# Gated-delta/pool decoder step: squares before norming, later roots, and another place for one weight block

## The chip, the cores and the metric

The kernel runs on one core of one Trainium2 chip. The metric is the device time of one execution in microseconds (us), as a median over runs; lower is better. Five engines of the core matter: TensorE (PE in the profile, with PEld for its weight loads), VectorE (DVE), ScalarE (ACT), GpSimd (POOL) and SyncE (SP), which only issues loads. Each works off its own list of instructions in order, and semaphores hold an instruction back until what it needs is there.

## The reference

One decoder layer runs over 512 prompt tokens and 8 sample tokens. A combined projection feeds a gated delta net and a pooling group, an output projection `W_out` adds to the residual `h`, and then comes the part at which the change sits:

```
h   = h + concat(dn_out, pool_out) @ w_out
xn2 = h * rsqrt(mean(h*h) + EPS) * norm_ffn         # RMSNorm over 2048 features
gu  = xn2 @ w_gate_up                               # 2048 -> 2 x 5632
h   = h + (silu(gu[:, :5632]) * gu[:, 5632:]) @ w_down
```

## The kernel before

**Layout and products.** Features lie on the 128 partitions, the 520 tokens along the free axis in two halves of 260. The residual stands in two tiles of eight feature rows each, `mixa` (the first 1024 features) and `mixb` (the others), `part(hk, half, ...)` picking tile and token half. Each float32 operand is split into a high part `hi` and a low part `lo` (`hi` is a cast on ACT, L1217 or L1535; `lo` a subtraction on DVE, L1218 or L1539). A product of one weight block (1024 x 128) with one form (1024 features x 260 tokens) is `passes`: eight steps of three matmuls (hi·hi, hi·lo, lo·hi, L1224 to L1226), so 24 matmuls of 128x260. A form that changes place in eight rows is made by `stream`: four pairs of rows, each with a DVE operation, a cast on ACT and a subtraction on DVE.

**The stages around the change.** The output projection ends with an output pair called `last`. Its second token half is finished from the banks `acc_c[0]` and `acc_c[1]`: `finish` (L1562) adds a bank to the residual (L1559, DVE), squares it (L1565, ACT) and stores it (L1566, a DMA on ACT's queue), and `total` (L1570, DVE) adds the squares to `sqa`. All squares share one buffer, so each square waits for the sum before it. For RMSNorm, `roots` (L1378) lets PE sum `sqa` over the partitions (L1383), DVE scale it (`sv`, L1387) and POOL take the power -1/2 (L227); `diagonals` (L1395, DVE, three pieces) and `spread` (L1401 on PE, L1402 on ACT) spread the result over partitions as `rb2`; `normed` (L1413, DVE) multiplies two rows of a half by it. `weighted` (L1408, ACT) puts the norm's weight on the last rows.

Then the gate and up projections begin. Pairs are `gu[0]` (gate, blocks `w0`) and `gu[1]` (up, blocks `w1`), called pair 0 and pair 1 here, each with blocks A11, A21, A12 and A22. They are worked off in plain products while the seven forms B11, B21, B22, T1, T2, T3 and T4 are built from the normed halves; from `gu[2]` on Strassen's seven products per pair run (M1, M4, M7, M6, M5, M2, M3 in this order). Of these, M4 is the first to read the form T4, with block A22 of `gu[2]`; M7 needs the sum block S3, for which A21 of `gu[2]` is loaded into rows of `mixb`, once the first cut of T4 has read them.

**Order.** No scheduler works here (`manual_schedule`): the order of the lines is the order on each engine.

**Places.** Blocks cut by `cut` go to the rotating tiles `hi`/`lo` of the pool `wpl` (three each), or to another pool if one is named. Pair 0's A22 is cut into the pool `sc0`, and before the change so is pair 1's A22, after it. `place` (L1527) instead writes the two parts of a block side by side into one tile of an old form. The old T4 of the output projection (`t4oh`, `t4ol`, pool `t4p`) holds pair 0's A11 and A21 in this way. When the plain products are issued, `p2a`, `sc0` and `t4p` are closed, and the new T4's high tile `T4h` is laid at bytes 129,728 to 138,048 of each partition; `sc0`'s high tile begins at 137,952, so that the two share 96 bytes. Its low tile `T4l` takes the place of `t4ol`. `t4oh` shares no byte with either.

Of the kernel before, what the change touches and what calls it, by code (L numbers as in the profile page):

```python
# [69 lines left out]
def decoder_kernel(ctx, tc, x_prompt, x_sample, state_delta, state_conv, state_pool, norm_mix, w_in,  # L70
# [17 lines left out]
    def pst():  # L88
        return ps_dn.tile([P, 512], F32, tag="dn", name="dn")
# [70 lines left out]
    def weights(view, K, parts=None):  # L160

        ng = -(-K // HG)
        sizes = [K // ng + (1 if i < K % ng else 0) for i in range(ng)]
        out = []
        k0 = 0
        for n in sizes:
            hi, lo = granule(view, k0, n, P, parts)
            for j in range(n):
                out.append((hi[:, j, :], lo[:, j, :]))
            k0 += n  # L170
        return out
# [38 lines left out]
    def part(hk, half, k0=0, k1=8):  # L210
        return (mixa, mixb)[hk][:, k0:k1, HALF * half:HALF * half + HALF]
# [54 lines left out]
    with tc.tile_pool(name="ph0", bufs=2) as ph0, tc.high_priority(offset=10 * AHEAD), tc.manual_schedule():  # L266
# [20 lines left out]
        def roots(ti, parts=1):  # L287
            s, r = ss0[:, 2 * ti:2 * ti + 1], rs0[:, ti:ti + 1]
            if parts == 2:
                dve.tensor_tensor(s, s, ss0[:, 2 * ti + 1:2 * ti + 2], op=ALU.add)  # L290
            dve.tensor_scalar(s, s, 1.0 / D, EPS, op0=ALU.mult, op1=ALU.add)
            pow_mhalf(r, s)
# [11 lines left out]
        class Block:  # L304
# [24 lines left out]
            def high(self):  # L329
                act.copy(self.hi, self.xm)  # L330

            def low(self, eng):
                eng.tensor_tensor(self.lo, self.xm, self.hi.bitcast(F32), op=ALU.subtract)  # L333
# [184 lines left out]
    with ExitStack() as p1:  # L518
# [625 lines left out]
        w = weights(w_out[0].rearrange("(k p) c -> p k c", p=P)[:, :, 8 * P:9 * P], KT)  # L1144
# [26 lines left out]
    def stacked(name, bufs=1, side="left"):  # L1171
        stack = ExitStack()
        return stack, stack.enter_context(tc.tile_pool(name=name, bufs=bufs, side=side, reuse_waits="tile"))
# [3 lines left out]
    def form_tiles(pool_, name):  # L1177
        return tuple(pool_.tile([P, 8, HALF], F32R, name=name + x) for x in "hl")

    b11, b21 = form_tiles(f12, "b11"), form_tiles(f12, "b21")  # L1180
    t4s, t4p = stacked("t4p", side="right")
    sc0s, sc0 = stacked("sc0", side="right")
# [7 lines left out]
    forms = {"B11": (xh[:, 0:8, 0:HALF], xl[:, 0:8, 0:HALF]), "B21": (xh[:, 8:16, 0:HALF], xl[:, 8:16, 0:HALF]),  # L1190
             "B22": (xh[:, 8:16, HALF:], xl[:, 8:16, HALF:]), "T1": (xh[:, 0:8, HALF:], xl[:, 0:8, HALF:]),
             "T2": b11, "T3": b21, "T4": form_tiles(t4p, "t4o")}
# [28 lines left out]
    def passes(acc, w, form, start=True, stop=True, ks=None):  # L1221
        (wh, wl), (xf, xg) = w, forms[form]
        for k in ks or range(wh.shape[1]):
            te.matmul(acc, wh[:, k, :], xf[:, k, :], start=start and k == 0, stop=False)  # L1224
            te.matmul(acc, wh[:, k, :], xg[:, k, :], start=False, stop=False)  # L1225
            te.matmul(acc, wl[:, k, :], xf[:, k, :], start=False, stop=stop and k == wh.shape[1] - 1)  # L1226
# [113 lines left out]
    def ffn_pair(fp, up):  # L1340
        return Pair(lambda i, j: wgv[:, 8 * j:8 * j + 8, up * FF + (2 * fp + i) * P:up * FF + (2 * fp + i + 1) * P],
                    up_out if up else gate_out)

    gu = [ffn_pair(fp, up) for fp in range(FP) for up in range(2)]
# [47 lines left out]
    def diagonals(rv):  # L1392
        dg = p2a.tile([P, HALF], F32, tag="dg", name="dg", bufs=1)
        for j, (t0, n) in enumerate(((0, P), (P, P), (2 * P, HALF - 2 * P))):
            dve.tensor_scalar(dg[:, t0:t0 + n], ident[:, P - n:P], rv[:, j:j + 1], None, op0=ALU.mult)  # L1395
        return dg
# [7 lines left out]
    def weighted(half):  # L1404

        for k in (6, 7):
            x = part(1, half)[:, k, :]
            act.activation(x, x, AF.Copy, scale=nffn(8 + k))  # L1408

    def normed(hk, half, k0, k1, eng=dve):  # L1410

        x, rb = part(hk, half, k0, k1), rb2[:, HALF * half:HALF * half + HALF]
        eng.tensor_tensor(x, x, rb.rearrange("p (o c) -> p o c", o=1).broadcast_to([P, k1 - k0, HALF]), op=ALU.mult)  # L1413
# [109 lines left out]
    acc_a, acc_b, acc_c = ([pst()[:, :HALF] for _ in range(2)] for _ in range(3))  # L1523
    w = last.w

    def place(pair, name, hold):

        hi, lo = (hold.rearrange("p k c -> p (k c)")[:, j * HG * P:(j + 1) * HG * P] for j in range(2))
        raw = pair.raw[name]
        act.copy(hi, raw)  # L1530
        dve.tensor_tensor(lo, raw, hi.bitcast(F32), op=ALU.subtract)
        pair.w[name] = [x.rearrange("p (k c) -> p k c", c=P) for x in (hi, lo)]
# [8 lines left out]
    def stream(name, src, make, lag=1):  # L1541

        for i in range(4 + lag):
            if i < 4:
                make(2 * i)
                high(name, src, 2 * i)
            if i >= lag:
                low(name, src, 2 * (i - lag))
# [8 lines left out]
    def add_to(i, half, acc):  # L1557
        x = mix[KT - 2 + i][:, HALF * half:HALF * half + HALF]
        dve.tensor_tensor(x, x, acc, op=ALU.add)  # L1559

    def finish(i, half, acc):
        c = slice(HALF * half, HALF * half + HALF)  # L1562
        add_to(i, half, acc)
        sq = p2.tile([P, NTOK], F32, tag="sq", name="sq")[:, c]
        act.activation(sq, mix[KT - 2 + i][:, c], AF.Square)  # L1565
        act.dma_start(h_d[KT - 2 + i][:, c], mix[KT - 2 + i][:, c])  # L1566
        return sq, c

    def total(sq, c):
        dve.tensor_tensor(sqa[:, c], sqa[:, c], sq, op=ALU.add)  # L1570
# [26 lines left out]
    gu[0].load("A22")  # L1597
    passes(acc_c[1], w["A21"], "T1", stop=False, ks=range(5, 8))
    passes(acc_c[0], w["A12"], "B22", start=False)
    forms["B11"] = b11  # L1600
    stream("B11", part(0, 0), lambda k: normed(0, 0, k, k + 2))
    gu[1].cut("A21")
    gu[1].load("A12")
    total(*finish(0, 1, acc_c[0]))
    passes(acc_c[1], w["A22"], "B22", start=False)
    f1 = finish(1, 1, acc_c[1])
    for k in (0, 2):
        normed(1, 0, k, k + 2)
    total(*f1)
    weighted(1)  # L1610

    xs_.close()
# [10 lines left out]
    def two():  # L1623
        return [pst()[:, :HALF] for _ in range(2)]

    c0 = [ps_mm.tile([P, HALF], F32, tag="mm", name="mm") for _ in range(2)]
    a0 = two()
    halves = slice(0, HALF), slice(HALF, NTOK)
    w0, w1 = gu[0].w, gu[1].w
    passes(a0[0], w0["A11"], "B11", ks=range(5))  # L1630
    rv = roots(1)
    for k in (4, 6):
        normed(1, 0, k, k + 2)
    passes(a0[0], w0["A11"], "B11", ks=range(5, 8))
    passes(a0[1], w0["A21"], "B11", ks=range(6))
    dg = diagonals(rv)
    spread(1, dg)
    for k in range(0, 8, 2):
        high("B21", part(1, 0), k)
        low("B21", part(1, 0), k)  # L1640
    passes(a0[1], w0["A21"], "B11", ks=range(6, 8))
    gu[0].cut("A12")
    gu[1].load("A22")
    a1 = two()
# [26 lines left out]
    stream("T3", part(0, 1), minus(part(0, 1), part(1, 1), part(0, 1)))  # L1671
    gu[1].cut("A12")
    gu[2].load("A22")
    passes(c0[0], w0["A12"], "B22", start=False)
    passes(c0[1], w0["A22"], "B22", start=False)
    stream("T2", part(1, 1), minus(part(1, 1), part(1, 1), part(0, 0)))
    for j in range(2):
        gate_out(j, 1, sg[:, j, halves[1]], c0[j])
    gu[2].cut("A11")
    gu[1].cut("A22", sc0)  # L1680
    h1 = two()
    passes(h1[0], w1["A12"], "B21")
    passes(c1[0], w1["A12"], "B22", start=False)
# [257 lines left out]
```

## Time and profile before

| | us |
|---|---|
| median of 3 runs (2198.1 to 2200.36) | 2199.5 |
| the profiled execution | 2196.74 |
| its span | 2195.0 |
| PE busy in the span | 2149.0 (98%) |
| DVE busy | 1735.2 (79%) |
| ACT busy | 955.0 (44%) |
| POOL busy | 462.9 (21%) |
| mean granted TensorE clock, as a share of full speed | 0.993 |

The span runs from the first to the last instruction; the execution's own time is 1.74 us longer. Times within the profile are in us from the span's start. The change lies between 795 and 885. A timeline row gives the start, the duration, the engine, the line, what is written from what, and in brackets the idle time before it with its inferred releaser.

### The profile page before, as it was taken

Reading aid. Unit: us, or ns where it says so; the run is one execution under the profiler, and the core shown is the slowest. Engines: PE = TensorE matmul, PEld = TensorE weight load, DVE = VectorE, ACT = ScalarE, POOL = GpSimd, SP = SyncE. Lnnn points to the kernel's source line nnn. Section 1 sums busy time; section 2 is a strip of 40 time slices with the busy share of each in tenths; the row PEclk is TensorE's granted clock in tenths of the full one; section 3 lists DMA queues with packets and bytes.
Section 4 is the critical chain, followed back from the end, with each engine's and each line's share of the span. In section 5 each row is a group of like instructions: output and inputs, shape, how many; then the busy total and the mean of one; then the engine's idle time right before and its main releaser. Section 6 shows DMA issues by size and latency. Waiting matters only on the chain.

```text
span 2195.0 us, 42970 instructions
## 1 busy us (share of the span) xinstructions
PE 2149.0 (98%) x17815; PEld 2141.4 (98%) x17815; DVE 1735.2 (79%) x2518; ACT 955.0 (44%) x1491; POOL 462.9 (21%) x520
## 2 busy tenths in 40 slices
PE   5999999999999998999999999999999999999998
PEld 5999999999999998999999999999999999999997
DVE  6676567566489968988898888888887798887996
ACT  5434453443255444433443433434434434435454
POOL 4111111001022210423323333232012402003110
PEclk8999999999999999999999999999999999999999
DMA  6443333323435442545455445545446837438333
GB/s 202 133 105 103 82 82 104 101 76 85 131 105 164 147 131 57 174 142 160 143 150 169 146 137 163 152 136 151 132 135 180 254 101 208 114 103 246 91 108 111
DMA packets 444728, 297.03 MB, mean 135 GB/s; under 512 B 26548, under 2 KB 424653, under 8 KB 441189
## 3 DMA queue, kind: packets, MB, share of 16 engines
q1 hardware_dynamic: 426661, 225.13, 36.3%
q0 software_dynamic: 16880, 68.51, 9.7%
q8 instruction: 139, 2.28, 0.4%
q10 hardware_dynamic: 992, 0.66, 0.1%
q14 instruction: 56, 0.46, 0.1%
HBM read 251.47 MB, written 43.43 MB: 134 GB/s over the span
## 4 chain that ended last, share of the span: by engine, by line
PE 92%; DVE 3%; ACT 1%; issue 1%; DMA 1%; POOL 0%; DVEq 0%; ACTq 0%
PE dn L1224 22%; PE dn L1225 22%; PE dn L1226 22%; PE mm L179 7%; PE mm L181 7%; PE mm L180 7%; PE dn L854 1%; DVE lo L1218 1%; ACT hi L1217 0%; PE dn L1849 0%; PE dn L774 0%; PE dn L964 0%; PE dn L900 0%; PE dn L861 0%; PE dn L836 0%
## 5 line engine op out<-in xcount | busy, mean ns | idle before, releaser
L1217 ACT CAST hi<-raw 128x1024 fp32r<-128x1024 f32 (+1 forms) x425 | 430.6, 1027 | 406.1 <-DVE raw L1246 211.2
L1218 DVE TENSOR_TENSOR lo<-raw,hi 128x1024 fp32r<-128x1024 f32 (+1 forms) x425 | 532.2, 1272 | 91.4 <-ACT hi L1217 89.7
L179 PE MATMUL mm<-xh,hi 128*128 128x256 f32 (+1 forms) x1280 | 379.7, 297 | 0.6 <-ACT ccs L735 0.6
L180 PE MATMUL mm<-xl,hi 128*128 128x256 f32 (+1 forms) x1280 | 362.1, 283 | 2.6 <-DVE xl L333 1.8
L181 PE MATMUL mm<-xh,lo 128*128 128x256 f32 (+1 forms) x1280 | 362.5, 283 | 0.2 <-DVE lo L148 0.2
L180 PEld LDWEIGHTS mm<-xl,hi 128*128 128x128 f32 x1280 | 242.9, 190 | 2.9 <-issue 1.9
L179 PEld LDWEIGHTS mm<-xh,hi 128*128 128x128 f32 x1280 | 242.6, 190 | 1.4 <-ACT ccs L735 0.7
L181 PEld LDWEIGHTS mm<-xh,lo 128*128 128x128 f32 x1280 | 241.7, 189 | 0.4 <-DVE lo L148 0.4
L1226 PE MATMUL dn<-b21h,lo 128*128 128x260 f32 x636 | 180.1, 283 | 0.9 <-DVE lo L1218 0.9
L1224 PE MATMUL dn<-b21h,hi 128*128 128x260 f32 x636 | 180.1, 283 | 0.0
L1225 PE MATMUL dn<-b21l,hi 128*128 128x260 f32 x636 | 179.5, 282 | 0.3 <-DVE b21l L1733 0.3
L1246 DVE TENSOR_TENSOR raw<-raw 128x1024 f32<-128x1024 f32 (+1 forms) x132 | 176.0, 1333 | 2.2
L1226 PE MATMUL dn<-b11h,lo 128*128 128x260 f32 x620 | 175.4, 283 | 0.0
L1224 PE MATMUL dn<-b11h,hi 128*128 128x260 f32 x620 | 175.4, 283 | 0.0
L1225 PE MATMUL dn<-b11l,hi 128*128 128x260 f32 x620 | 174.9, 282 | 0.0
L148 DVE TENSOR_TENSOR lo<-raw,hi 128x1024 fp32r<-128x1024 f32 (+1 forms) x86 | 102.6, 1197 | 75.0 <-ACT hi L146 74.9
L1224 PE MATMUL dn<-T1h,hi 128*128 128x260 f32 x564 | 160.2, 284 | 0.0
L1225 PE MATMUL dn<-T1l,hi 128*128 128x260 f32 x564 | 159.9, 284 | 0.0
L1224 PE MATMUL dn<-B22h,hi 128*128 128x260 f32 x564 | 159.8, 283 | 0.0
L1225 PE MATMUL dn<-B22l,hi 128*128 128x260 f32 x564 | 159.5, 283 | 0.0
L1226 PE MATMUL dn<-T1h,lo 128*128 128x260 f32 x564 | 158.9, 282 | 0.0
L1226 PE MATMUL dn<-B22h,lo 128*128 128x260 f32 x564 | 158.5, 281 | 0.0
(578 smaller groups left out, 6425.3 us busy)
## 6 DMA issues: line engine op xcount, KB each, us to landing
raw<-in_w_gate_up_dram SPq DMA_DIRECT2D x134, 512.0 KB
raw<-in_w_in_dram SPq DMA_DIRECT2D x80, 512.0 KB
a_d<-mixa POOLq DMA_DIRECT2D x22, 1040.0 KB, 5.5
mixb<-in_w_gate_up_dram SPq DMA_DIRECT2D x42, 512.0 KB
raw<-in_w_down_dram SPq DMA_DIRECT2D x48, 448.0 KB
raw<-in_w_out_dram SPq DMA_DIRECT2D x25, 512.0 KB
st<-a_d POOLq DMA_DIRECT2D x49, 260.0 KB, 6.4
raw<-in_w_down_dram SPq DMA_DIRECT2D x24, 512.0 KB
```

Source lines behind the costliest of these rows:

```text
L148: dve.tensor_tensor(lo[:, :f], raw[:, :f], hi[:, :f].bitcast(F32), op=ALU.subtract)
L179: te.matmul(acc[ci], wh, hi[k][:, c0:c1], start=(k == 0), stop=False)
L180: te.matmul(acc[ci], wh, lo[k][:, c0:c1], start=False, stop=False)
L181: te.matmul(acc[ci], wl, hi[k][:, c0:c1], start=False, stop=(k == len(w) - 1))
L854: te.matmul(yp[:, ck(c)], xt_[:, ck(c)], cur[:, ck(c)], start=True, stop=True)
L1217: act.copy(hi, raw)
L1218: dve.tensor_tensor(lo, raw, hi.bitcast(F32), op=ALU.subtract)
L1224: te.matmul(acc, wh[:, k, :], xf[:, k, :], start=start and k == 0, stop=False)
L1225: te.matmul(acc, wh[:, k, :], xg[:, k, :], start=False, stop=False)
L1226: te.matmul(acc, wl[:, k, :], xf[:, k, :], start=False, stop=stop and k == wh.shape[1] - 1)
L1246: dve.tensor_tensor(r[name], r[a], r[b], op=op)
```

## The change

Three things change.

1. In the second half of the output projection's last pair, both `finish`/`total` steps come before pair 1's A21 is cut and before any norming of half 1 of B21; the cut, the load of A12 and one norming step (two rows) follow. One norming step moves behind the request for the roots.
2. The request for the roots of half 1 comes after all eight steps of the product A11·B11 of pair 0, not after five; the spreading of the result after seven steps of the next product, not six.
3. Pair 1's A22 is written into `t4oh` by `place`, ahead of the building of T2, not cut into `sc0` after it.

```diff
-    forms["B11"] = b11
+    forms["B11"], held = b11, forms["T4"]
     stream("B11", part(0, 0), lambda k: normed(0, 0, k, k + 2))
+    total(*finish(0, 1, acc_c[0]))
+    passes(acc_c[1], w["A22"], "B22", start=False)
+    total(*finish(1, 1, acc_c[1]))
     gu[1].cut("A21")
     gu[1].load("A12")
-    total(*finish(0, 1, acc_c[0]))
-    passes(acc_c[1], w["A22"], "B22", start=False)
-    f1 = finish(1, 1, acc_c[1])
-    for k in (0, 2):
-        normed(1, 0, k, k + 2)
-    total(*f1)
+    normed(1, 0, 0, 2)
     weighted(1)
...
-    passes(a0[0], w0["A11"], "B11", ks=range(5))
+    passes(a0[0], w0["A11"], "B11")
     rv = roots(1)
-    for k in (4, 6):
+    for k in (2, 4, 6):
         normed(1, 0, k, k + 2)
-    passes(a0[0], w0["A11"], "B11", ks=range(5, 8))
-    passes(a0[1], w0["A21"], "B11", ks=range(6))
+    passes(a0[1], w0["A21"], "B11", ks=range(7))
     dg = diagonals(rv)
     spread(1, dg)
...
-    passes(a0[1], w0["A21"], "B11", ks=range(6, 8))
+    passes(a0[1], w0["A21"], "B11", ks=range(7, 8))
...
     gu[1].cut("A12")
     gu[2].load("A22")
+    place(gu[1], "A22", held[0])
...
     gu[2].cut("A11")
-    gu[1].cut("A22", sc0)
```

On DVE, from the end of the form B11 to the pieces of the diagonal (`lo<-raw,hi` is pair 1's A21, `sqa` the sum of squares, `rb_7798` the spread roots of half 0):

```order
 L1539 TENSOR_TENSOR b11l<-mixa,b11h 128x520 x2
-L1218 TENSOR_TENSOR lo<-raw,hi 128x1024
 L1559 TENSOR_TENSOR mixb<-mixb,dn 128x260
 L1570 TENSOR_TENSOR sqa<-sqa,sq 128x260
 L1559 TENSOR_TENSOR mixb<-mixb,dn 128x260
-L1413 TENSOR_TENSOR mixb<-mixb,rb_7798 128x2x260 x2
 L1570 TENSOR_TENSOR sqa<-sqa,sq 128x260
+L1218 TENSOR_TENSOR lo<-raw,hi 128x1024
+L1413 TENSOR_TENSOR mixb<-mixb,rb_7798 128x2x260
 L1387 TENSOR_SCALAR sv<-dn 128x3
-L1413 TENSOR_TENSOR mixb<-mixb,rb_7798 128x2x260 x2
+L1413 TENSOR_TENSOR mixb<-mixb,rb_7798 128x2x260 x3
```

Three operations leave the way to the second sum; two of them now stand between it and `sv`, and one more between `sv` and the diagonal.

On ACT, from the casts of T3 to those of T4 (`hi<-raw` are casts of weight blocks, `t4oh<-raw` that of pair 1's A22):

```order
 L1535 CAST T3h<-mixa 128x520 x4
 L1217 CAST hi<-raw 128x1024
+L1530 CAST t4oh<-raw 128x1024
 L1535 CAST T2h<-mixb 128x520 x4
 L1335 ACTIVATE sg<-sg 128x260 x2
-L1217 CAST hi<-raw 128x1024 x2
+L1217 CAST hi<-raw 128x1024
 L1535 CAST T4h<-mixb 128x520 x4
```

One cast moves ahead of T2's; the count of instructions ahead of T4's casts stays the same. On DVE the block's subtraction moves in the same way.

## Rows read from the trace of the kernel before

**Rows 1.** The page: busy time, share of the span and instructions of each engine.

```profile
PE 2149.0 (98%) x17815; PEld 2141.4 (98%) x17815; DVE 1735.2 (79%) x2518; ACT 955.0 (44%) x1491; POOL 462.9 (21%) x520
```

**Rows 2.** Stretches: from:to, length, then PE, PEld, DVE, ACT, POOL busy; PEclk; DMA.

```profile
960.00:1200.00 240.00, 240.00 (x1996) 239.90 (x1995) 209.32 (x221) 95.81 (x118) 76.37 (x60) 1.00 0.51 150
...
808.00:814.00 6.00, 6.00 (x29) 6.00 (x29) 2.00 (x6) 1.02 (x2) 1.17 (x1) 0.50 0.01 3
...
52.00:56.00 4.00, 2.63 (x19) 2.34 (x20) 0.09 (x1) 1.39 (x4) 2.11 (x3) 1.00 1.07 287
```

**Rows 3.** Timeline of PE, 795 to 883: start, duration, instruction, idle before and releaser.

```profile
807.10 1.17 PE L1383 MATMUL dn<-ones,sqa 128*128 128x2 f32 x6 [3.97 <-DVE sqa L1570]
...
814.12 0.64 PE L1401 MATMUL dn<-dg,ones 128*128 128x260 f32 x2
...
828.81 0.39 PE L1225 MATMUL mm<-T1l,t4oh 128*128 128x260 f32 x1 [0.24 <-DVE T1l L1539]
...
851.95 0.39 PE L1226 MATMUL dn<-b21h,lo 128*128 128x260 f32 x1 [0.94 <-DVE lo L1218]
...
862.62 0.39 PE L1224 MATMUL dn<-T4h,hi 128*128 128x260 f32 x1 [2.03 <-ACT hi L1217]
...
865.88 0.59 PE L1226 MATMUL dn<-T4h,lo 128*128 128x260 f32 x1 [2.75 <-DVE lo L1218]
...
881.73 0.28 PE L1226 MATMUL dn<-B22h,lo 128*128 128x260 f32 x1
```

**Rows 4.** Timeline of DVE, 800 to 810: the sums and the roots of half 1.

```profile
800.85 1.48 DVE L1539 TENSOR_TENSOR b11l<-mixa,b11h 128x520 fp32r<-128x520 f32 x2
...
803.72 0.42 DVE L1559 TENSOR_TENSOR mixb<-mixb,dn 128x260 f32<-128x260 f32 x1
804.62 0.43 DVE L1570 TENSOR_TENSOR sqa<-sqa,sq 128x260 f32<-128x260 f32 x1 [0.48 <-ACT sq L1565]
...
806.53 0.42 DVE L1570 TENSOR_TENSOR sqa<-sqa,sq 128x260 f32<-128x260 f32 x1
808.30 0.16 DVE L1387 TENSOR_SCALAR sv<-dn 128x3 f32<-128x3 f32 x1 [1.35 <-PE dn L1383]
...
809.81 0.62 DVE L1395 TENSOR_SCALAR dg<-ident,rv 128x128 f32<-128x128 f32 x3
```

**Rows 5.** Timeline of ACT, 801 to 858.

```profile
801.50 1.04 ACT L1217 CAST hi<-raw 128x1024 fp32r<-128x1024 f32 x1
...
805.48 0.42 ACT L1565 ACTIVATE sq<-mixb 128x260 f32<-128x260 f32 x1 [0.89 <-DVE mixb L1559]
...
808.12 1.17 ACT L1408 ACTIVATE mixb<-mixb,prm 128x260 f32<-128x260 f32 x2 [2.22 <-DMA h_d<-mixb]
...
857.78 1.15 ACT L1535 CAST T4h<-mixb 128x520 fp32r<-128x520 f32 x2 [7.33 <-PE dn L1226]
```

**Rows 6.** Timeline of DVE, 842 to 882: T2, T4 and the blocks of gu[2].

```profile
842.12 1.30 DVE L1553 TENSOR_TENSOR mixb<-mixb,mixa 128x520 f32<-128x520 f32 x2
843.51 0.70 DVE L1539 TENSOR_TENSOR T2l<-mixb,T2h 128x520 fp32r<-128x520 f32 x1
...
851.81 1.30 DVE L1553 TENSOR_TENSOR mixb<-mixb 128x520 f32<-128x520 f32 x2
858.43 0.70 DVE L1539 TENSOR_TENSOR T4l<-mixb,T4h 128x520 fp32r<-128x520 f32 x1 [5.32 <-ACT T4h L1535]
...
863.13 1.22 DVE L1246 TENSOR_TENSOR mixb<-raw,mixb 128x1024 f32<-128x1024 f32 x1 [0.77 <-DMA mixb<-in_w_gate_up_dram]
...
864.61 1.22 DVE L1218 TENSOR_TENSOR lo<-raw,hi 128x1024 fp32r<-128x1024 f32 x1
...
879.72 2.36 DVE L1218 TENSOR_TENSOR lo<-raw,hi 128x1024 fp32r<-128x1024 f32 x2 [1.43 <-ACT hi L1217]
```

**Rows 7.** The chain that ended last: start, length and what, loads alone.

```profile
859.16 3.94 DMA mixb<-in_w_gate_up_dram
...
1743.30 7.10 DMA raw<-in_w_down_dram
```

## The prediction

> **What bounds the kernel now.** I read the page's engine table first: PE is busy for 2149.0 of 2195.0 us [rows 1], so only time that PE loses can be won. Over a steady stretch it runs 1996 matmuls in 240 us without a gap, one per 0.120 us, at the full clock of 2.4 GHz [rows 2]. Then I read PE's timeline where the change sits, for gaps. There are five [rows 3]: 3.97 us before the sums over `sqa` at 807.10, 0.24 at 828.81 (T1's low part), 0.94 at 851.95 (pair 1's A22, low part), and 2.03 and 2.75 in M4, at 862.62 and 865.88 (block A22 of `gu[2]`, high and low part). After the first gap the granted clock is 0.50 (the level of 1.2 GHz): 29 matmuls take 6.00 us [rows 2]. So two places lose time: the roots of half 1, and the start of M4. Each is the end of a chain over DVE and ACT, so the question is how much earlier these chains end.
>
> **Part 1, the squares and the roots.** PE asks for the sums before DVE has made them. Before, the second sum starts at 806.53, and PE follows 0.57 us later [rows 3, 4]. Ahead of the sums DVE has a block's low part and two norming steps, which now come after.
>
> The new chain on DVE: B11 ends at 800.85 + 1.48 = 802.33 [rows 4]. From the first addition to its sum of squares it takes 804.62 - 803.72 = 0.90, the square on ACT included. The sum itself takes 0.43 and then the second addition begins, since one buffer serves all squares. So the second sum starts at 802.33 + 0.90 + 0.43 + 0.90 = 804.56, and PE's sums at about 805.13.
>
> PE arrives there when? Its gap began at 807.10 - 3.97 = 803.13, after five of eight steps; three more steps are nine matmuls of 0.120, or 1.08 us, so it arrives at 804.21. A gap of 0.9 us stays, where 3.97 was.
>
> But DVE now has two operations ahead of `sv`. ACT casts A21 after the second square, which ends near 804.5; the cast takes 1.04 [rows 5], so DVE's subtraction runs from about 805.6 for 1.22 (the same form at 864.61 [rows 6]), to 806.8. One norming step takes 0.65 (half of 1.30, by the like form of T2 at 842.12 [rows 6]), to 807.45, and then comes `sv`. The way from `sv` to the diagonal over POOL took 809.81 - 808.30 = 1.51 [rows 4], to about 809.0; meanwhile DVE norms three times, 1.95, to 809.55. The diagonal takes 0.62, and PE spreads at about 810.2. In the x2 rows neighbours overlap by about 0.1 us, over some five places 0.4 us; I take 810.0. It was 814.12 [rows 3].
>
> PE itself is there earlier: sums of at most 1.17 us and 21 matmuls at 0.120 (2.52) give 808.8, so it waits 1.2 us for the diagonal, a gap which it did not have. It costs nothing beyond 810.0, as DVE and ACT set what follows: T1, through `rb2`, follows the spreading at the same distance as before, and PE already waited 0.24 for T1 [rows 3]; it now waits about 0.7, as three matmuls fewer lie between. **Term 1: 814.1 - 810.0 = 4.1 us**, with 3.4 (if the roots' way over POOL or the cast is slower by half a us) and 4.6 (all overlaps for the good) as ends. ACT's weighting now stands behind the cast; it starts 808.12 - 805.48 = 2.64 after the second square, when the store has landed [rows 5], so at about 806.8, ends near 808, and ACT copies `rb2` after 810: two us of cover. The load of pair 1's A12 waits for A21's raw tile, some 3 us longer against its old place; its cast comes after those of T1, B22 and T3, later than 828.81 [rows 3], so some 20 us on.
>
> **Part 2, pair 1's A22.** The block's cast (1.04) and subtraction (1.22) are not new, only earlier, between T3 and T2, so both engines have the same work ahead of T4. The 0.94 at 851.95 goes. What matters is T4. ACT's first cast of T4 waited 7.33 us until PE had ended, to 857.78 [rows 5]; that end is the last product with pair 1's A22, since `T4h` shares 96 bytes with the tile in which that block lay. DVE had been ready for T4 since 851.81, and lost 5.32 us before the first low part at 858.43 [rows 6]. With the block in `t4oh` that tile's last reader is pair 0's A22, whose product with B22 stands four products (96 matmuls, 11.5 us) earlier on PE.
>
> So T4 runs as T2 ran: the first low part starts 843.51 - 842.12 = 1.39 us after the first subtraction [rows 6], at 853.20 instead of 858.43. **Term 2: 5.2 us** on top of term 1. What is late next: the load of A21 of `gu[2]` into `mixb` may start once this first part has read its rows. It took 3.94 us [rows 7], and S3 started at 863.13, 4.70 after that first part [rows 6]. That stays, so S3, and A22's low part behind it on DVE, come 5.2 earlier as well: at 859.4 instead of 864.61, still in the old times. PE reaches M4 at 862.62 - 2.03 - 0.94 = 859.65 and needs the low part at its third matmul, 865.88 - 864.61 = 1.27 after that subtraction starts, so at 860.65. It still waits some 0.8 us, so term 2 is set by DVE and the load, not by the sum of PE's gaps (5.7). Its ends: 4.2, should the load be a quarter slower, and 5.7.
>
> **Part 3, behind M4.** Without the long gaps PE should run M4 to M3 at full clock: 120 matmuls, 14.4 us, from the third of M4 to the third of M3. Before, this took 881.73 - 865.88 = 15.85 us [rows 3]. But the third of M3 needs the low part of S4, the first of two at 879.72; it ends 879.72 + 1.2 - 864.61 = 16.3 us after A22's subtraction starts [rows 6], while PE would be there at 1.27 + 14.4 = 15.7. So a new gap of 0.7 us opens there, and of the 17.1 us between 864.61 and 881.73 only **term 3: 0.7 us** is won (ends 0 and 1.4).
>
> **Sum:** 4.1 + 5.2 + 0.7 = 10.0 us. From there to the end PE is the bound [rows 1, 2], with nothing tied to absolute time, so the lead stays. The span goes from 2195.0 to 2185.0, the profiled execution from 2196.74 to 2186.7. The median shown lies 2.76 us above that execution; I carry that over, 2199.5 - 10.0 = 2189.5.
>
> **A rule weighed.** At full clock PE's time between 52 and 56 was busy for only 2.63 of 4.00 us, and the granted clock stayed at 1.00 [rows 2]; of the clock's falls near the change, one came after the gap of 3.97. The Trainium skill, "TensorE: Matmul & The Clock Gate", section "A second HAM failure mode: psum-queue depth-cycling", speaks against this change: a PE that idles often for short moments between groups of matmuls is throttled again and again. By that rule the short gaps that replace the long one (0.9 and 1.2 us, with 2.5 us of matmuls between) would bring the low clock as well; the stretch at 52 does not agree, and no run here shows this pattern near 805.
>
> **The rivals.**
>
> *The clock falls on the short gaps.* The low level costs 6.00/29 - 0.120 = 0.087 us a matmul [rows 2]. Against it stands the stretch at 52. Over some 30 matmuls on both sides of the spreading it is 2.6 us; of this the wait for T1 (0.7) and that in M4 (0.8) take up 1.5. So 1 to 2 us are lost: 2190.5 to 2191.5.
>
> *T4 stays bound.* If something else in `T4h`'s place is read as late as the last product, the change does not do what it says: M4's gaps stay but for the 0.94 that PE arrives earlier. Then 4.1 + 0.9 = 5.0 is won: 2194.5. Against it: the tiles that share its bytes hold squares, `sqa`, the roots and pair 0's A22, all read long before.
>
> *The load for S3 is slower.* It may meet others' traffic; a load of the chain took 7.10 us [rows 7], 3.16 more than this one. Then term 2 is 2.0: about 2192.7.
>
> *Slower than before.* The stores of half 1 could land late: ACT holds `rb2`'s copy behind the weighting, which waits for them. Landing takes 2.64 us from the square now; with 2 us of cover, time is lost from 4.6 us on, and the kernel is slower than before from 4.6 + 10.0 = 14.6 us. At 16 us it would take 2200.9. Nothing near that is seen: the wait was 2.22 [rows 5].
>
> **How the numbers follow.** Forecast 0.77; clock 0.10; T4 bound 0.05; slower load 0.06; late stores 0.02. The ends of the terms give 3.4 + 4.2 + 0 = 7.6 and 4.6 + 5.7 + 1.4 = 11.7 us won, thus 2187.8 to 2191.9; the runs shown differ by about 1 us from their median, so I take 2187.0 to 2192.8, which takes in the clock and the slower load too, and leaves out T4 bound and the late stores with tails of the rest. A measurement of this kernel can tell about 0.2%, 4.4 us, from no change. Faster by more than that, all cases but the late stores and some of T4 bound: 0.94; within 0.2%: 0.04; slower: 0.02.
>
> **What would show it.** PE's timeline after: a gap near 804 of about 1 us instead of 3.97, the sums over `sqa` near 805, the spreading near 810 after a new gap of about 1.2, granted clock 1.00 throughout. T4's first cast on ACT following DVE without the wait on PE; S3 released by its load; in M4 one gap of under 1 us at the third matmul, in M3 one of about 0.7. Wrong would be a granted clock of 0.50 near 806 to 812, a T4 cast released by PE, or gaps of PE behind M3, which would give the lead back.

## The result and the profile after

The changed kernel takes 2188.4 us in the median of 4 runs (2185.7 to 2189.3), the kernel before 2198.8 us in the 4 runs beside it: a ratio of 0.995, with a 95% interval of 0.993 to 0.997, or 10.4 us less. Forecast were 2189.5 us and a lead of 10.0. The profiled execution of the changed kernel took 2189.26 us with a span of 2187.3, so the two profiled spans lie only 7.7 us apart. What takes the rest is seen below.

The page's engine table, which answers to [rows 1]:

```profile
PE 2143.5 (98%) x17815; PEld 2135.1 (98%) x17815; DVE 1731.4 (79%) x2518; ACT 955.6 (44%) x1491; POOL 465.5 (21%) x520
```

The instruction counts are the same. Over the whole span PE is busy for 5.5 us less and idle for 43.8 us instead of 46.0.

**PE around the change.** Timeline of PE of the changed kernel: start, duration, instruction, and in brackets the idle time before it with its releaser. The first row is the first matmul of pair 0's A11·B11, with which the changed stretch begins.

```profile
802.77 0.28 PE L1224 MATMUL dn<-b11h,t4oh 128*128 128x260 f32 x1
...
806.66 0.80 PE L1383 MATMUL dn<-ones,sqa 128*128 128x2 f32 x6 [0.85 <-DVE sqa L1570]
...
811.48 0.70 PE L1401 MATMUL dn<-dg,ones 128*128 128x260 f32 x2 [1.39 <-DVE dg L1395]
...
826.23 0.39 PE L1225 MATMUL mm<-T1l,t4oh 128*128 128x260 f32 x1 [0.56 <-DVE T1l L1539]
...
858.45 0.39 PE L1226 MATMUL dn<-T4h,lo 128*128 128x260 f32 x1 [1.52 <-DVE lo L1218]
...
873.58 0.39 PE L1226 MATMUL dn<-B22h,lo 128*128 128x260 f32 x1 [0.43 <-DVE lo L1218]
```

Against [rows 3]: the gap of 3.97 at the sums has become one of 0.85 and a new one of 1.39 at the spreading; the one of 0.94 at pair 1's A22 is gone; M4's two, 2.03 and 2.75, have become one of 1.52; and M3 has a new one of 0.43.

Start-up differs between executions. The stretch's first matmul starts at 802.77 here and started at 801.15 in the kernel before, and the sums of half 0 (L1383), ahead of all that changed, stand 10.45 us before it in both; so the profiled execution after was 1.62 us late before any changed instruction ran. The row of the kernel before:

```profile
801.15 0.28 PE L1224 MATMUL dn<-b11h,t4oh 128*128 128x260 f32 x1
```

I therefore measure distances from that first matmul. It reads, before and after: to the spreading 12.97 and 8.71, to the third matmul of M4 (`T4h,lo`) 64.73 and 55.68, to the third of M3 (`B22h,lo`) 80.58 and 70.81. The stretch is 9.77 us shorter; less the 1.62 of the start, and 0.45 that the executions differ behind M3, this is the 7.7 of the spans. The medians, 10.4 apart, agree with the stretch.

Of the 9.77, 5.2 are idle time of PE (9.93 to 4.75 us in the stretch). The other 4.6 are busy time (70.65 to 66.06 us) for the same work, which before ran in part at the low clock.

**DVE at the roots**, the timeline that answers to [rows 4]:

```profile
802.47 1.48 DVE L1539 TENSOR_TENSOR b11l<-mixa,b11h 128x520 fp32r<-128x520 f32 x2
803.87 0.42 DVE L1559 TENSOR_TENSOR mixb<-mixb,dn 128x260 f32<-128x260 f32 x1
...
806.09 0.43 DVE L1570 TENSOR_TENSOR sqa<-sqa,sq 128x260 f32<-128x260 f32 x1 [0.55 <-ACT sq L1565]
807.15 1.22 DVE L1218 TENSOR_TENSOR lo<-raw,hi 128x1024 fp32r<-128x1024 f32 x1 [0.64 <-ACT hi L1217]
808.30 0.69 DVE L1413 TENSOR_TENSOR mixb<-mixb,rb 128x520 f32<-128x520 f32 x1
808.91 0.15 DVE L1387 TENSOR_SCALAR sv<-dn 128x3 f32<-128x3 f32 x1
808.98 1.91 DVE L1413 TENSOR_TENSOR mixb<-mixb,rb 128x520 f32<-128x520 f32 x3
810.81 0.61 DVE L1395 TENSOR_SCALAR dg<-ident,rv 128x128 f32<-128x128 f32 x3
```

The second sum now follows B11 by the squares alone. After it DVE waits 0.64 for ACT's cast of A21, then works without a break to the diagonal, which frees PE at 811.48.

**T4 and the blocks of `gu[2]`**, for [rows 5, 6]: first ACT's cast of T4, then DVE's timeline, then the load of A21 in the chain of waits (start, length, what), which answers to [rows 7].

```profile
850.03 1.17 ACT L1535 CAST T4h<-mixb 128x520 fp32r<-128x520 f32 x2 [1.98 <-DVE mixb L1553]
```

```profile
849.23 1.31 DVE L1553 TENSOR_TENSOR mixb<-mixb 128x520 f32<-128x520 f32 x2
850.70 0.70 DVE L1539 TENSOR_TENSOR T4l<-mixb,T4h 128x520 fp32r<-128x520 f32 x1 [0.16 <-ACT T4h L1535]
...
855.70 1.22 DVE L1246 TENSOR_TENSOR mixb<-raw,mixb 128x1024 f32<-128x1024 f32 x1 [1.08 <-DMA mixb<-in_w_gate_up_dram]
...
857.18 1.22 DVE L1218 TENSOR_TENSOR lo<-raw,hi 128x1024 fp32r<-128x1024 f32 x1
...
872.30 2.36 DVE L1218 TENSOR_TENSOR lo<-raw,hi 128x1024 fp32r<-128x1024 f32 x2 [1.43 <-ACT hi L1217]
```

```profile
851.42 4.25 DMA mixb<-in_w_gate_up_dram
```

ACT's cast, which waited 7.33 us for PE, now waits for DVE, and DVE's 5.32 us before the first low part are 0.16. What sets S3 is the load. The last row is the pair of low parts whose first, S4's, frees M3.

**The clock.** Three stretches of the changed kernel: from:to, length, busy time of PE, PEld, DVE, ACT and POOL, PEclk, DMA.

```profile
806.00:808.00 2.00, 1.34 (x12) 1.37 (x12) 1.27 (x2) 1.96 (x4) 0.00 (x0) 1.00 0.22 71
...
810.00:812.00 2.00, 0.61 (x4) 0.49 (x3) 1.42 (x5) 0.00 (x0) 0.38 (x1) 1.00 0.75 222
...
857.00:859.00 2.00, 0.55 (x4) 0.55 (x5) 2.00 (x4) 1.04 (x1) 0.00 (x0) 1.00 0.00 0
```

The granted clock is 1.00 (2.4 GHz) at these three gaps, and in the whole stretch. Before, it was 0.50 from 807.4 to 814.2 and again from 865.4 to 868.8.

### The profile page after: what moved, and what is told of

It is laid out like the page before. It is cut to its first block, busy times and chain, and to the rows that moved or that the text cites. A ratio compares the mean times of both kernels' runs of the same rounds, so it can differ in the third digit from the quotient of the medians.

```text
span 2187.3 us, 42971 instructions
## 1 busy us (share of the span) xinstructions
PE 2143.5 (98%) x17815; PEld 2135.1 (98%) x17815; DVE 1731.4 (79%) x2518; ACT 955.6 (44%) x1491; POOL 465.5 (21%) x520
## 4 chain that ended last, share of the span: by engine, by line
PE 88%; DVE 4%; ACT 2%; issue 1%; DMA 1%; POOL 0%; SPq 0%; DVEq 0%; ACTq 0%; POOLq 0%
PE dn L1224 21%; PE dn L1225 21%; PE dn L1226 21%; PE mm L179 7%; PE mm L181 6%; PE mm L180 6%; DVE lo L1218 1%; PE dn L854 1%; DMA st<-a_d 1%; ACT hi L1217 1%; DVE raw L1246 0%; PE dn L1846 0%; PE dn L964 0%; PE dn L861 0%; PE dn L900 0%
## 5 line engine op out<-in xcount | busy, mean ns | idle before, releaser
L1354 POOL TENSOR_TENSOR mixa<-mixa 128x520 f32<-128x520 f32 x22 | 50.8, 2309 | 499.9 <-DVE mixa L1348 499.9
```

Of the source, the lines that this page charges most:

```text
L1354: pool.tensor_tensor(q[:, 4:8:2, :], q[:, 1:4:2, :], q[:, 0:2, :], op=ALU.subtract)
```

## The experiments

Each was timed beside the kernel before on the same chip; a run's number is that of its paragraph. "Stretch" means the distance from the first matmul of A11·B11 to the third of M3: 80.58 before, 70.81 after. The theory: the lead is made of three waits, at the roots, at T4 (the bytes that it shares) and at M3. The rivals: one part makes all of it, or the gaps matter through the clock and not through their length. M3 has no run of its own; it is read from the traces of the others.

**1. The squares and roots without the new place.**

```diff
 (changed kernel)
-    place(gu[1], "A22", held[0])
...
     gu[2].cut("A11")
+    gu[1].cut("A22", sc0)
```

> The squares go ahead of the norming and the roots are asked for later, as in the change, but pair 1's A22 is cut into sc0 at its old place. The stretch measured is from PE's first matmul of pair 0's A11 with B11 to the third matmul of M3: 80.58 us before, 70.81 with the whole change. My theory (DVE and ACT chains set both ends, the two parts add up): term 1 alone, the spreading 8.7 us after the stretch's start (12.97 before), M4's gaps of 2.0 and 2.8 stay with T4's first cast released by PE, the clock falls there once more; stretch 76.3, time 4.3 under before, about 2194.5. Rival (what counts is PE's gap and the low clock after it, and both come back to the end): 3.1 of the gap plus 2.7 of the clock, stretch 74.8, 5.8 under before.

Measured: 2194.3 us against 2198.7, ratio 0.998 (0.997 to 0.999), 4.3 us less; the stretch is 76.80. The spreading comes at 8.70, as in the full change. PE, in M4, and DVE, at T4:

```profile
861.66 0.54 PE L1224 MATMUL dn<-T4h,hi 128*128 128x260 f32 x1 [2.04 <-ACT hi L1217]
...
865.12 0.58 PE L1226 MATMUL dn<-T4h,lo 128*128 128x260 f32 x1 [2.70 <-DVE lo L1218]
```

```profile
857.47 0.70 DVE L1539 TENSOR_TENSOR T4l<-mixb,T4h 128x520 fp32r<-128x520 f32 x1 [5.32 <-ACT T4h L1535]
```

M4's gaps and DVE's wait of 5.32 stand as in [rows 3, 6]: the lead of the roots is carried through, and T4 stays bound. The half us over the expected 76.3 goes with the clock, which here was low for 6.8 us from M4's first gap on, twice as long as before.

**2. The place alone.**

```diff
 (kernel before)
-    forms["B11"] = b11
+    forms["B11"], held = b11, forms["T4"]
...
+    place(gu[1], "A22", held[0])
...
-    gu[1].cut("A22", sc0)
```

> Pair 1's A22 lies in t4oh, ahead of T2, as in the change; sums, norming and roots stand as before. My theory: term 1 is lost, terms 2 and 3 stay. The gap of 4.0 before the sums and the low clock behind it are there, the spreading 13.0 us after the stretch's start; T4's first cast is not released by PE; M4 has one gap of about 1.5. Stretch 80.58 - 5.5 = 75.1, time about 5.5 under before, 2193.3. Rival (T4 would have been late anyway, its gaps are the roots' lateness): stretch over 78.

Measured: 2192.6 us, ratio 0.9975 (0.996 to 0.999), 6.0 us less; stretch 74.94. PE:

```profile
808.37 1.41 PE L1383 MATMUL dn<-ones,sqa 128*128 128x2 f32 x6 [3.97 <-DVE sqa L1570]
...
862.25 0.39 PE L1226 MATMUL dn<-T4h,lo 128*128 128x260 f32 x1 [1.90 <-DVE lo L1218]
```

The gap of 3.97 stays and M4 has its one gap. The spreading comes at 12.57, not at the 13.0 expected: the low clock, again 6.8 us long, began at 807.4, inside the gap, so that less of PE's work fell into it. In the medians 4.3 and 6.0 make 10.3, against 10.4 for the whole change; in the stretch 3.78 and 5.64 make 9.42, against 9.77. The parts add up to within half a us, and neither makes all of the lead.

**3. The gap at the roots filled.** In the kernel before, 28 more matmuls stand ahead of the sums of half 1. They write a bank that the sums and nothing else use, and what they write is read by nothing. DVE's and ACT's work is untouched.

```diff
 (kernel before, in roots)
+        for j in range(28 * half):
+            te.matmul(pn[:, 16:16 + HALF], gu[0].w["A11"][0][:, j % 4, :], b11[0][:, j % 4, :], start=True, stop=True)
```

> The kernel before, but with 28 more matmuls of 128x260 on PE right ahead of the sums over sqa of half 1, whose results nothing reads; they take 3.4 us and fall into the gap of 4.0. They cost no time where they stand, and show what the low clock behind the gap cost by itself. If the clock holds because PE is busy: granted 1.00 from 803 on; 27 matmuls from the sums to the spreading take 3.2 instead of about 6, so the spreading comes 10.1 us after the stretch's start instead of 12.97, and 2.9 us of the 4.3 of term 1 are the clock's; time 2.9 under before. If the chain over DVE alone set the spreading: 12.97 as before, no gain. M4's gaps stay as before in both.

Measured: 2195.3 us, ratio 0.9987 (0.9977 to 0.9997), 3.4 us less although PE has more to do. Its timeline, and a stretch of it with the columns as above:

```profile
803.60 3.48 PE L1383 MATMUL dn<-b11h,t4oh 128*128 128x260 f32 x28
...
807.66 0.83 PE L1385 MATMUL dn<-ones,sqa 128*128 128x2 f32 x6 [0.58 <-DVE sqa L1572]
...
811.68 0.60 PE L1403 MATMUL dn<-dg,ones 128*128 128x260 f32 x2
```

```profile
808.00:810.00 2.00, 2.00 (x19) 2.00 (x19) 1.38 (x3) 1.03 (x2) 1.17 (x1) 1.00 0.22 72
```

The clock stays at 1.00 up to M4, and the spreading comes 9.88 after the start, where it took 12.97. So 3.1 of the 4.3 us that the change wins at the roots were lost not in the wait but at the 1.2 GHz behind it: here the second rival is right for the larger part. Up to M4's third matmul the lead is 3.1; at M3 2.3 is left, since the low clock behind M4's gaps lasted 6.8 us here too.

**4. The same move to another old tile.** The block goes into `t4ol`, whose place the new `T4l` takes.

```diff
 (changed kernel)
-    place(gu[1], "A22", held[0])
+    place(gu[1], "A22", held[1])
```

> The whole change, but pair 1's A22 is placed in t4ol, whose bytes the new T4's low tile takes, not in t4oh. It is cut at the same early time. My theory (what counts is which tile its last product keeps busy): T4's casts go ahead, but DVE's first low part of T4 waits for PE's last product with that block, about 856.9 in times of before, so some 1.4 us earlier than before instead of 5.2; load, S3 and A22 follow it. M4's gap grows to about 4 to 5 us in all, the clock may fall there; stretch about 74.5, time about 2192.5. Rival (the earlier cut alone wins term 2): stretch 70.8 as with the change.

Measured: 2193.0 us, ratio 0.9974 (0.996 to 0.998), 5.6 us less; stretch 75.56. DVE at T4:

```profile
853.63 0.70 DVE L1539 TENSOR_TENSOR T4l<-mixb,T4h 128x520 fp32r<-128x520 f32 x1 [3.43 <-PE dn L1226]
```

T4 waits for PE again, now by its low tile. Order and work are those of the changed kernel; only the bytes differ. That makes the shared bytes the cause. `t4oh` and `t4ol` lie in one pool, which is closed at the same line in both runs, so the closing of a pool does not make the wait. It is held for a whole tile: `T4h`'s 96 shared bytes lie in the last of its eight rows, and yet in the kernel before the cast of its first two waited. The clock was low for 6.8 us at M4's gaps (1.44 and 2.82), and from M4's third matmul to M3's third it took 16.84, where the kernel before took 15.85; that is the us above the expectation.

**5. The new place at the old time.** The block is written into `t4oh` after T2, where the cut stood.

```diff
 (changed kernel)
-    place(gu[1], "A22", held[0])
...
     gu[2].cut("A11")
+    place(gu[1], "A22", held[0])
```

> The whole change, but pair 1's A22 is placed in t4oh at the old time, after gu[2]'s A11, not ahead of T2. My theory (the place wins, not the time): T4's first cast is still not released by PE and T4 starts as with the change; PE's gap of 0.9 at A22's low part returns, but is taken from the gap in M4 (1.5 to about 0.6), so the stretch stays at 70.8 and the time is that of the change. Rival (the time wins): T4 or M4 later by 0.9 or more, stretch 71.7 or more.

Measured: 2187.4 us, ratio 0.9953 (0.994 to 0.997), beside runs of the kernel before at 2197.6; stretch 70.50. PE:

```profile
848.51 0.39 PE L1226 MATMUL dn<-b21h,t4oh 128*128 128x260 f32 x1 [0.95 <-DVE t4oh L1531]
```

The gap of 0.95 is back, and M4's gap has gone altogether (its third matmul comes at 55.37, with no idle time before it). It costs nothing at M3, which waits 0.44 for S4's low part as in the changed kernel, so that DVE behind the load still sets it. In this run the load took 3.96 us instead of 4.25, which is the 0.3 by which the stretch is shorter. The earlier time of the block, as distinct from its place, gained nothing.

**6. The roots asked for after five steps again**, and the spreading after six; all else as changed. Two runs.

```diff
 (changed kernel)
-    passes(a0[0], w0["A11"], "B11")
+    passes(a0[0], w0["A11"], "B11", ks=range(5))
     rv = roots(1)
...
-    passes(a0[1], w0["A21"], "B11", ks=range(7))
+    passes(a0[0], w0["A11"], "B11", ks=range(5, 8))
+    passes(a0[1], w0["A21"], "B11", ks=range(6))
```

> The whole change, but PE asks for the sums after five steps of A11 with B11, and for the spreading after six steps of A21, as before. My theory (the order on DVE and ACT is what wins, PE's place of asking only moves a gap): the gap before the sums grows from 0.85 to about 1.9, the one before the spreading shrinks from 1.4 to 0.3; the spreading stays 8.7 us after the stretch's start and the stretch at 70.8 (plus 0.3 for three matmuls more behind the spreading, hidden by T1). Same time as with the change. Rival (asking later wins): the gap of 1.9 costs 1.1 us more, stretch 71.9, and 73 or more if the granted clock falls behind it.

> The kernel with the roots asked for early (after five and six steps) once more, as its first profile showed the granted clock at 0.50 for 3.4 us behind its gap of 1.9 and again in M4, where the change kept 1.00. If the low clock comes with the longer gap: low again behind the sums, the spreading 9.3 us after the stretch's start, stretch 72 to 73. If it was a matter of the single execution: clock 1.00 throughout, the spreading at 8.7, stretch 70.8.

Measured: 2188.6 us (ratio 0.9958, 0.994 to 0.997) and 2189.0 (0.9954, 0.994 to 0.997). PE of the first run, and a stretch of it with the columns as above:

```profile
805.93 0.80 PE L1383 MATMUL dn<-ones,sqa 128*128 128x2 f32 x6 [1.92 <-DVE sqa L1570]
```

```profile
808.00:810.00 2.00, 2.00 (x12) 2.00 (x11) 2.00 (x5) 0.00 (x0) 1.18 (x1) 0.52 0.53 153
```

A gap of 1.9 at the sums brought the clock down for 3.4 us, in both runs. The spreading comes at 9.34 and 9.40, some 0.65 later than in the changed kernel, but T1 then waits only 0.22 instead of 0.56, and at M3 the second run is 0.4 late. In the first, M4's gap of 1.89 brought a second low period, and M3 is 1.9 late (72.73). So the theory's 8.7 at the spreading was wrong, and the fall of the clock, on the rival's side, came. The times cannot be told from the changed kernel's; the traces can. Asking three steps later is worth little time here and keeps the clock up.

**7. The changed kernel once more**, beside the runs that follow.

> The whole change once more, beside the three that follow, for a comparison on the same chip: stretch 70.8, about 10 us under before.

Measured: 2187.7 us against 2198.4, ratio 0.9955 (0.994 to 0.997); gaps 1.39, 0.58, 1.50 and 0.43, clock at 1.00, stretch 70.78. The picture of the first profile repeats to some hundredths.

**8. A shorter chain at the roots.** DVE norms twice ahead of `sv`, while ACT casts A21, and makes the low part while POOL takes the power.

```diff
 (changed kernel)
     total(*finish(1, 1, acc_c[1]))
-    gu[1].cut("A21")
-    gu[1].load("A12")
-    normed(1, 0, 0, 2)
-    weighted(1)
+    for k in (0, 2):
+        normed(1, 0, k, k + 2)
...
     rv = roots(1)
-    for k in (2, 4, 6):
-        normed(1, 0, k, k + 2)
+    gu[1].cut("A21")
+    gu[1].load("A12")
+    weighted(1)
...
     dg = diagonals(rv)
+    for k in (4, 6):
+        normed(1, 0, k, k + 2)
```

> The whole change, with DVE's order around the roots turned once more: after the second sum two norming steps, then sv, then pair 1's A21 (whose cast on ACT goes ahead of the weighting), then the diagonal, and the last two norming steps behind it. My theory (the spreading is set by DVE's two operations ahead of sv and the three behind it): the diagonal follows POOL at once, the spreading comes 1.4 us earlier, 7.3 after the stretch's start; stretch 69.4. Rival (POOL or PE sets the spreading, or the two norming steps behind the diagonal hold up the casts of B21 by as much): 8.7, or 7.3 with the stretch still at 70.8.

Measured: 2185.8 us, ratio 0.9942 (0.993 to 0.996); stretch 69.91. DVE now waits for POOL at the diagonal:

```profile
809.12 0.62 DVE L1395 TENSOR_SCALAR dg<-ident,rv 128x128 f32<-128x128 f32 x3 [0.74 <-POOL rv L227]
```

The spreading comes at 7.58 (1.13 earlier than in the changed kernel), and M3 0.9 earlier. So the gap of 1.39 was worth about 1.1, as a chain of DVE, not as PE's. The 1.4 expected fell short by what POOL then holds up, and the load, at 4.49 us, took another quarter of a us before M3.

**9. A22 of `gu[2]` cut ahead of S3.**

```diff
 (changed kernel)
+    gu[2].cut("A22")
     gu[2].add("S3")
     up_out(0, 0, cm[:, 0, :], h1[0])
-    gu[2].cut("A22")
```

> The whole change, with A22 of gu[2] cut before S3 is formed, so that DVE makes A22's low part while the load for S3 is under way. My theory (M4 waits for DVE behind that load, and M3 for the chain from S3 to S4): M4's gap of 1.5 goes to under 0.3; the chain from S3 to S4 has one operation less in it, M3's third matmul comes 1.1 earlier, where a gap of about 1 us stands; stretch 69.7. Rival (M3's gap grows by what M4's shrinks): stretch 70.8.

Measured: 2188.5 us, ratio 0.9956 (0.994 to 0.997); stretch 71.21, longer than the 70.78 beside it. M4 has no gap, but three others opened, one in M6 and two in M3:

```profile
862.13 0.39 PE L1226 MATMUL dn<-T2h,lo 128*128 128x260 f32 x1 [0.93 <-DVE lo L1218]
...
871.00 0.39 PE L1224 MATMUL dn<-B22h,hi 128*128 128x260 f32 x1 [0.18 <-ACT hi L1217]
872.27 0.39 PE L1226 MATMUL dn<-B22h,lo 128*128 128x260 f32 x1 [0.76 <-DVE lo L1218]
```

My theory here, that the lead at M4 is kept, fell. DVE shows why:

```profile
856.77 1.23 DVE L1218 TENSOR_TENSOR lo<-mixb,hi 128x1024 fp32r<-128x1024 f32 x1 [0.58 <-ACT hi L1217]
...
863.15 3.47 DVE L1218 TENSOR_TENSOR lo<-raw,hi 128x1024 fp32r<-128x1024 f32 x2
866.65 1.65 DVE L1246 TENSOR_TENSOR raw<-raw 128x1024 f32<-128x1024 f32 x1
```

A22's low part had filled the time in which DVE waits for S3's cast; taken away, that wait (0.58) is open, and ahead of S3 the low part holds S3 itself up by 0.3. The pair of low parts starts 14.17 after T4's first low part, where it was 14.32: 0.15 gained of an operation's 1.13. The pair then takes 3.47 us instead of 2.35, beside POOL (below). Between M4 and M3 DVE has no spare time, so moving work within it moves the gaps.

**10. Both together**, the edits of runs 8 and 9.

> Both turns of the two kernels above together. My theory: they add up, 1.4 + 1.1 = 2.5 us under the change, stretch 68.3, time about 12.5 under before. Rival: one hides the other, stretch 69.4 or more.

Measured: 2186.6 us, ratio 0.995 (0.994 to 0.996); spreading 7.59, stretch 70.09, gaps 0.93, 0.20 and 0.76 as in run 9. No better than run 8 alone, as the rival had it.

**11. Run 8 with A21 of `gu[2]` loaded ahead**, into a tile of its own, at bytes that are free by then, so that S3 waits for no load.

```diff
 (run 8)
+    r2s, r2p = stacked("r2x", side="right")
+    r2t = r2p.tile([P, HG * P], F32, name="r2x")
+    r2p.tile([P, 2080], F32, name="r2y")
+    gu[2].load("A21", r2t)
     stream("T4", part(1, 0), minus(part(1, 0), part(1, 0), part(1, 1)))
-    gu[2].load("A21", fb[:, 0:1024])
...
     up_out(1, 1, cm[:, 1, :], c1[1])
+    r2s.close()
```

> The kernel with DVE's order around the roots turned, and the load of A21 of gu[2] goes to a tile of its own that is free since pair 0's A22 was last read, so that it need not wait for T4's first low part. If the load is what M4 waits for (my theory): it lands before T4 is done, S3 follows T4 at once, 1.1 to 1.3 us earlier; M4's gap goes from 1.8 to about 0.5, stretch 68.7 instead of 69.9, time about 1 us lower than without. Rival (DVE is slowed beside POOL in turn, as where A22 was cut first): M4's gap shrinks, but M3's third matmul comes at most 0.4 earlier, stretch 69.5 or more.

Measured: 2186.3 us against 2198.4, ratio 0.9943 (0.993 to 0.996); stretch 68.49, the shortest of all. DVE and PE:

```profile
853.89 1.22 DVE L1246 TENSOR_TENSOR r2x<-raw,r2x 128x1024 f32<-128x1024 f32 x1
```

```profile
856.63 0.39 PE L1226 MATMUL dn<-T4h,lo 128*128 128x260 f32 x1 [0.35 <-DVE lo L1218]
```

S3 follows T4 without a wait, and M4's gap falls to 0.35. By the trace this beats the change by 2.3 us. The medians of runs 8 and 11 (0.994 of the kernel before) lie 1.4 to 1.9 us under that of run 7, but all intervals overlap, so a gain over the change is shown by the traces only, one profile of each.

## Why the prediction was right

**Term 1, the roots: 4.1 forecast, 4.26 measured** (12.97 to 8.71). With the late start of 1.62 added to the forecast's times, the chain fits link by link: sums at 806.75 forecast and 806.66 measured, `sv` at 809.07 and 808.91, the diagonal at 811.17 and 810.81, the spreading at 811.6 and 811.48. The gaps, 0.9, 1.2 and 0.7 (T1) forecast, are 0.85, 1.39 and 0.56. The new end was right because DVE set it, as worked out. The old end was misread: the prediction takes both places for ends of chains over DVE and ACT, but before the change DVE's diagonal had ended at 809.81 + 0.62 = 810.43 [rows 4], and PE spread at 814.12 without a wait [rows 3], after its own matmuls at 1.2 GHz. The sum did not suffer, since it subtracts a time worked out from a time read. What the clock had cost was left out of the term; run 3 shows that 3.1 of the 4.26 could be had by keeping PE busy, with DVE as it was.

**Term 2, T4: 5.2 forecast, 4.79 measured**, from the spreading to A22's low part (50.49 to 45.70). The cause was right: runs 4 and 5 show that the bytes decide and the time of the block does not. T4's first low part came 5.09 earlier, 0.1 short of the forecast. The mis-sized step is the load, taken at 3.94: it took 4.25. Over the runs it took 3.96 to 4.64, where I had taken one row for a constant; the lower end of 4.2 covered that. M4's gap, forecast at 0.8, is 1.52: the low part came 0.4 later than forecast and PE 0.3 earlier. A gap costs PE more than its idle time, since the matmul behind it takes 0.39 us where the others take 0.28; the working had taken off the idle time alone for the two gaps that went.

**Term 3, behind M4: 0.7 forecast, 0.72 measured** (17.12 to 16.40). S4's low part set M3 as said: it starts 872.30 - 857.18 = 15.12 after A22's, before it was 15.11. The gap is 0.43 instead of 0.7, since PE took 14.7 us from M4's third matmul to M3's third (873.58 - 858.45 - 0.43), where 120 times 0.120 had made 14.4. That 0.72 meets 0.7 so closely has some luck in it: the time before, 15.85 from M4's third matmul to M3's, is of one profile with a low clock of 3.4 us; with like gaps and 6.8 us of it, runs 1 and 3 took 16.07 and 16.68.

**Sum and median.** 9.77 in the stretch against 10.0, as term 1 came out 0.2 above and term 2 0.4 below. The median is 1.1 under the forecast of 2189.5: 0.7 because the median of the kernel before moved from 2199.5 to 2198.8 with its fourth run, 0.4 by the lead. Behind M3 PE is bound as before and the lead stays, but for 0.45 us; run 7's profile of the same kernel is 1.1 shorter there than the first, so this is no loss by the change. The waits of PE from 780 on, by line, what they waited for, total, count and longest, show that no new one of size stands behind M3 (those left out are of 0.4 us and less):

```profile
PE dn L1226 <- DVE lo L1218: 2.1, 3, 1.5
PE dn L1401 <- DVE dg L1395: 1.4, 1, 1.4
PE dn L1383 <- DVE sqa L1570: 0.8, 1, 0.8
PE mm L1225 <- DVE T1l L1539: 0.6, 1, 0.6
```

**The rivals.** The clock did not fall on the short gaps: 1.00 throughout the stretch in both profiles of the changed kernel. The rule that I weighed, of the Trainium skill, "TensorE: Matmul & The Clock Gate", section "A second HAM failure mode: psum-queue depth-cycling", was thus not borne out by gaps of 0.85 and 1.39 us. The rival was nearer than I gave it: with the one gap of 1.9 in run 6 the clock did fall, twice in two runs. T4 staying bound is what run 4 brought about: its stretch is 5.02 shorter than before, where 5.0 was worked out for this case, and its time is 2193.0 against 2194.5. The slower load came as a third of a us, not as 3.2. Late stores were not seen: ACT's weighting follows the cast without a wait.

```profile
807.03 0.96 ACT L1408 ACTIVATE mixb<-mixb,prm 128x260 f32<-128x260 f32 x2
```

## What to carry to other kernels

When the engine that bounds a kernel waits, follow the chain over the other engines to where it starts, and forecast the new end of that chain; the gap itself says neither what can be won (M4's 4.78 us of gaps gave way to one of 1.52) nor what it costs (behind the one of 3.97 a low clock cost 3.1 us by itself). Tiles laid over the bytes of older ones make waits that stand in no line of the program: 96 shared bytes held T4 for 5 us, and another free tile removed that without any change of the work. Where an engine off the critical path has no spare time left, as DVE between M4 and M3, moving its work about moves the gaps; take away a wait (the load in run 11, the cast's in run 8) instead.

## What the runs showed of the hardware

**The clock.** With the gap of 3.97 the granted clock fell to 1.2 GHz for 6.8 us, in the kernel before and in run 2. Gaps of 1.9 at the sums brought it to that level for 3.4 us in two profiles of two; a gap of 1.9 in M4 did so in the first profile of run 6 and not in run 2. M4's pair of gaps brought a low period in each of four profiles: 3.4 us long in the kernel before, 6.8 in runs 1, 3 and 4. Single gaps in M4 of 1.3 to 1.8 us never did (both profiles of the changed kernel, run 8, the second of run 6). So the same gap of about 2 us brought the low clock in one execution and not in another; in M4 this cost run 6's first profile 1.0 us up to M3 against its second (16.10 and 15.13).

**DVE and POOL side by side.** POOL's step at L1354 took 3.29 us in the changed kernel and 2.16 in run 9, though it began 0.2 us after the same DVE operation in both:

```profile
865.24 3.29 POOL L1354 TENSOR_TENSOR mixa<-mixa 128x520 f32<-128x520 f32 x1 [54.86 <-DVE mixa L1348]
```

```profile
863.38 2.16 POOL L1354 TENSOR_TENSOR mixa<-mixa 128x520 f32<-128x520 f32 x1 [54.72 <-DVE mixa L1348]
```

The difference, 1.13, is just what one DVE operation of 128x1024 takes from start to start, and in run 9 DVE's pair of low parts grew by 1.12. In the changed kernel the DVE operation that comes next, while POOL is still at its step, took 2.21 us, where the like operation at 861.59 took 1.22:

```profile
867.40 2.21 DVE L1246 TENSOR_TENSOR raw<-raw 128x1024 f32<-128x1024 f32 x1
```

Whole operations seem to stand aside for one another. The Trainium skill, "SBUF — State Buffer", section "SBUF: two separate sides", describes this: a VectorE operation with two inputs in SBUF and a GpSimd one that reads SBUF share a pair of ports, and whichever starts first holds it for the whole instruction. The trace agrees in these numbers; POOL's spans are rough, and no run here was made for it.

**A load's own spread.** The same load of A21 into `mixb` took from 3.94 to 4.64 us in the eleven profiles in whose chain it stands. Where a load ends last in a chain, as at S3, this spread is carried into the kernel's time.
